# A hybrid decoder block on one core: the first layer norm's residuals, PSUM banks and POOL's row work rearranged

## The chip, the cores and the metric

The kernel runs on one core of a Trainium2 chip. Its engines are TensorE (PE in the profile: matrix products, with its weight loads on a row PEld), VectorE (DVE), ScalarE (ACT), GpSimd (POOL) and SyncE (SP, which here only issues DMAs). The metric is the device time of one execution in microseconds; the figure of a kernel is the median of its runs.

## The reference

One decoder layer for 256 tokens of 1024 features, float32. The change touches the end of the mixing part and the start of the feed-forward part (FFN):

```python
x = layer_norm(ALPHA * x + y @ w_out, ln1_g, ln1_b)       # mean and variance over 1024 features
u = causal_dwconv(x @ ffn_w_up, ffn_conv_w) + ffn_conv_b   # 3 taps along the tokens, 2 * 2816 columns
u_gate, u_val = split(u, 2)
f = (silu(u_gate) * u_val) @ ffn_w_down
x = layer_norm(ALPHA * x + f, ln2_g, ln2_b)
```

Ahead of that, `y` is the gated sum of a gated delta rule and a sparse attention over the same tokens.

## The kernel before

**Products.** Each float32 operand is split into a high part (`hi`, rounded to the type fp32r) and a low part (`lo`, what is left), and a product is done as three: hi by hi, hi by lo, lo by hi. Weights come from memory in chunks of 128x1024 (512 KB) in the order of a list, `PLAN`, through six buffers `raw`. `split_chunk` makes the parts: ACT casts `raw` to `hi` (L187) and DVE subtracts (L192); for some chunks POOL does a share of the subtraction (L194). `ahead()` splits the chunks that come next, as long as no more than three pairs (`hi`, `lo`) are in use; its argument `most` limits how many. Two sorts of chunks don't count: those with a place of their own (`alt`), and the first FFN pair `ug` 0 and `uv` 0 (`plain`), which is multiplied unsplit.

**Order.** Everything is unrolled, and each engine runs its own instructions in the order of the program. An instruction waits only for the data or the buffer that it needs from another engine. A DMA is issued by its engine's queue in the same way.

**Out projection (L1115 to L1141).** The result is two row tiles (`t`, 128 tokens each) by two halves of 512 features (`hf`), four PSUM tiles `pwo` from a pool `s` of four buffers. Eight chunks `wo` follow each other: four for half 0 with both row tiles, then four for half 1 with row tile 0 (L1141), and the same four with row tile 1 (three at L1187, the last at L1192). `resid` (L1130, L1131) adds ALPHA times the input row to the product, into `res` (tile NQ), and takes its statistics. It is called for (0, half 0) and (1, half 0) at L1139, and for half 1 inside `norm1`.

**First norm (L1172 to L1206).** `norm1(t)` finishes row tile t's statistics and normalizes half of it on DVE (L1174) and half on ACT. `trans1` transposes the row tile on TensorE into two PSUM tiles `pxt` of the pool `s` (L1154). `evac1` scales and shifts them into `x1T` (tile AT; DVE at L1162, ACT at L143), and `hilo1` makes the parts for the FFN (cast on ACT L1169, difference L1170 on POOL, for one piece on DVE). `first_up` (L1183) is the product of the unsplit pair with one row tile; its two results `pg0` lie in the two buffers of the PSUM pool `g`. At the end POOL scales and shifts the normalized rows for the second residual, `x1` (L1205, L1206): four operations of 128x1024. They read `res` and the tile KD; `x1` is read first after the FFN. SP's load of the second norm's constants (L1209) stands behind them in the program.

**FFN (L1244 to L1272).** 22 rounds j. A round multiplies two chunks, `ug` and `uv`, with all tokens (24 products each, L316 to L318, result in the pool `g`), convolves each (ACT takes the first tap at L143, DVE the two others at L349, reading PSUM and SBUF), and splits further chunks. ACT applies SiLU, DVE multiplies the two (L1263), ACT casts the result (L1267), DVE makes its low part (L1268). Then `down(j - 1)` (L1227 to L1229) multiplies the result of the round before with chunk `dn`, 15 products into five PSUM tiles, four from the pool `s` and one from the pool `o` of one buffer. The pool `c` has one buffer too; the attention was the last to use it.

Of the kernel before, what the change touches and what calls it, by code (L numbers as in the profile page):

```python
# [6 lines left out]
F32 = mybir.dt.float32  # L7
# [3 lines left out]
OP = mybir.AluOpType  # L11
# [85 lines left out]
class Body:  # L97
# [894 lines left out]
    def run(self):  # L992
        nc, A = self.nc, self.A
# [80 lines left out]
        xk = V.rearrange("p h t -> p (h t)").rearrange("p (t d) -> p t d", t=2)  # L1074
# [9 lines left out]
        lnp = self.KD.rearrange("p u j -> p (u j)")[:, :2048].rearrange("p (n d) -> p n d", n=2)  # L1084
# [23 lines left out]
        res = self.NQ.rearrange("p h t -> p (h t)").rearrange("p (t d) -> p t d", t=2)  # L1108
        x1 = self.LT[:, :2048].rearrange("p (t d) -> p t d", t=2)
        x1T = self.AT[:, 0:2048].rearrange("p (k t) -> p k t", k=8)  # L1110
        pw = {}
# [3 lines left out]
        def wo_mm(hf, i, ts):  # L1115
            if (hf, i) not in ch:
                ch[hf, i] = [c.rearrange("p (k n) -> p k n", k=2) for c in self.next_chunk("wo", 4 * hf + i)]
            hi, lo = ch[hf, i]
            for t in ts:
                self.mm_tok([pw[t, hf]], hi, lo, Y, 2 * i, i == 0, i == 3, t)  # L1120
            if ts[-1] == 1:
                self.done_chunk("wo", 4 * hf + i)
                if hf == 0:
                    self.ahead()

        def resid(t, hf, x, p):
            sl = slice(512 * hf, 512 * hf + 512)
            if hf == 0:
                bn[t] = self.work.tile([128, 2, 6], F32, name="bn", bufs=2)
            nc.vector.scalar_tensor_tensor(res[:, t, sl], x[:, t, sl], ALPHA, p[t, hf], op0=OP.mult, op1=OP.add)  # L1130
            nc.vector.bn_stats(bn[t][:, hf], res[:, t, sl])  # L1131

        for hf in range(2):
            for t in range(2):
                pw[t, hf] = self.ps("pwo")
        for i in range(4):
            wo_mm(0, i, (0, 1))
        for t in range(2):
            resid(t, 0, xk, pw)  # L1139
        for i in range(4):  # L1140
            wo_mm(1, i, (0,))  # L1141
        g1, b1 = self.pp("g1"), self.pp("b1")

        def stats1(t):
            resid(t, 1, xk, pw)
            return self.ln_stats(bn[t])
# [20 lines left out]
        def hilo1(t, k0, n, eng):  # L1167
            ts, ks = slice(128 * t, 128 * t + 128), slice(k0, k0 + n)
            nc.scalar.copy(X[:, 0, ks, ts], x1T[:, ks, ts])  # L1169
            eng.tensor_tensor(X[:, 1, ks, ts], x1T[:, ks, ts], X[:, 0, ks, ts].bitcast(F32), op=OP.subtract)  # L1170

        def norm1(t):  # L1172
            rs, nm = stats1(t)
            nc.vector.tensor_scalar(res[:, t, :512], res[:, t, :512], rs, nm, op0=OP.mult, op1=OP.add)  # L1174
            self.act(res[:, t, 512:], res[:, t, 512:], AF.Identity, scale=rs, bias=nm)

        pg0 = [self.ps_g() for _ in range(2)]

        def first_up(w, t):
            wt = up0[w].rearrange("p (k m) -> p k m", k=8)  # L1180
            ts = slice(128 * t, 128 * t + 128)
            for k in range(8):
                nc.tensor.matmul(pg0[w][:, ts], wt[:, k], x1T[:, k, ts], start=(k == 0), stop=(k == 7))  # L1183

        norm1(0)
        for i in range(WO_T):
            wo_mm(1, i, (1,))  # L1187
        p0 = trans1(0, (0, 1))
# [12 lines left out]
        evac1(1, 1, p1[1], nc.vector)  # L1201
        for q in range(2):
            hilo1(1, 4 * q, 4, (nc.gpsimd, nc.vector)[q])
        for t in range(2):
            nc.gpsimd.tensor_tensor(x1[:, t], res[:, t], lnp[:, 0], op=OP.mult)  # L1205
            nc.gpsimd.tensor_tensor(x1[:, t], x1[:, t], lnp[:, 1], op=OP.add)  # L1206

        ln2 = self.AT[:, 2048:4096].rearrange("p (n d) -> p n d", n=2)
        nc.sync.dma_start(ln2.rearrange("p n d -> p (n d)"),  # L1209
# [13 lines left out]
        def down_mm(j, n):  # L1223
            (hi, lo), (fh, fl), (t, o, w) = dch[j], fs[j], parts[n]
            ts, sl = slice(128 * t, 128 * t + 128), slice(o, o + w)
            p = pd[n][:, :w]
            nc.tensor.matmul(p, fh[:, ts], hi[:, sl], start=(j == 0), stop=False)  # L1227
            nc.tensor.matmul(p, fh[:, ts], lo[:, sl], start=False, stop=False)  # L1228
            nc.tensor.matmul(p, fl[:, ts], hi[:, sl], start=False, stop=(j == NFF - 1))  # L1229

        def down(j, ns=range(5)):
            if j == 0:
                for n in range(4):
                    pd[n] = self.ps("pdn")
                pd[4] = self.psum.tile([128, 512], F32, name="pdn", tag="o", bufs=1)
            if j not in dch:
                dch[j] = self.next_chunk("dn", j)
            for n in ns:
                down_mm(j, n)
            if ns[-1] == 4:  # L1240
                self.done_chunk("dn", j)
                self.ahead(most=1 if j > NFF - 4 else 3)

        for j in range(NFF):  # L1244
            uu = []
            for w, n in enumerate(("ug", "uv")):
                if j:
                    hi, lo = self.next_chunk(n, j)
                    pg = self.mm_feat(hi, lo, X)
                    self.done_chunk(n, j)  # L1250
                else:
                    first_up(w, 1)
                    self.done_chunk(n, 0)
                    pg = pg0[w]
                c = w * NFF + j
                u = self.scr(n)[:, :256]
                self.conv(pg, u, fcw[:, c], fcb[:, c:c + 1])
                uu.append(u)
                if j + w < NFF:
                    self.ahead(most=1 if j > NFF - 4 else 3)  # L1260
            self.act(uu[0], uu[0], AF.Silu)
            f = uu[0]
            nc.vector.tensor_tensor(f, uu[0], uu[1], op=OP.mult)  # L1263
            if j == NFF - 1:
                self.ahead(most=1)
            fh, fl = Y[:, 0, j % 5], Y[:, 1, j % 5]
            nc.scalar.copy(fh, f)  # L1267
            nc.vector.tensor_tensor(fl, f, fh.bitcast(F32), op=OP.subtract)  # L1268
            fs[j] = (fh, fl)
            self.ahead(most=1 if NFF - 1 > j > NFF - 4 else 3)  # L1270
            if 0 < j < NFF - 4:
                down(j - 1)  # L1272
        self.tab(AF.Exp)
        N = NFF
        last = range(N - 5, N)
# [188 lines left out]
```

## Time and profile before

| | |
|---|---|
| median of 3 runs | 586.69 us (585.82 to 587.82) |
| profiled execution: its span, the only time given of it | 585.1 us |
| TensorE busy | 565.1 us (97%) |
| VectorE busy | 395.9 us (68%) |
| ScalarE busy | 301.8 us (52%) |
| GpSimd busy | 110.7 us (19%) |

The span runs from the first to the last instruction; the time of a run includes what lies around it. Busy time of TensorE is modelled, and its products overlap: one starts before the one ahead of it has ended. In a line of a view, `out<-in` names the tiles, `xN` is the number of instructions merged into it, and the square bracket holds the idle time of that engine just before and what ended it. Times in the timelines are from the span's start.

### The profile page before, as it was taken

To read this page: it belongs to the slowest core of one execution; us is meant where nothing else is said; L and a number is where in the kernel's file an instruction comes from. 1 tells how busy PE (TensorE), PEld (TensorE's weight loads), DVE (VectorE), ACT (ScalarE), POOL (GpSimd) and SP (SyncE) were. 2 spreads that over 40 slices of the span, in tenths; PEclk is the share of its full clock that TensorE was granted. 3 is DMA by queue.
4 is the path that set the end of the run, shared out by engine and by line. 5 is a ranking of instruction groups with operands and counts; after the bars stand their busy time and mean duration, and the time that the engine had idled before them with its cause. 6 is when DMAs were issued, how large, how long until landed. Compare 5 with 4: busy or idle time off the path is not lost.

```text
span 585.1 us, 11569 instructions
## 1 busy us (share of the span) xinstructions
PE 565.1 (97%) x4588; PEld 510.4 (87%) x4588; DVE 395.9 (68%) x674; ACT 301.8 (52%) x550; POOL 110.7 (19%) x127
## 2 busy tenths in 40 slices
PE   8999999999989999999999999969999999999993
PEld 6999988878989998878979898769999999999983
DVE  1888743684986643576666486787777677777886
ACT  3655643424464475555685344355555555555651
POOL 1466611406310120020000000171000000000053
PEclk9999999999999999999999999998999999999998
DMA  8975578874953242323445455544555555555501
GB/s 267 408 253 173 171 233 263 298 231 148 273 168 103 85 134 79 102 73 109 146 146 169 162 183 194 190 135 130 190 188 187 180 184 190 192 189 183 181 2 72
DMA packets 29798, 101.87 MB, mean 174 GB/s; under 512 B 3536, under 2 KB 5360, under 8 KB 29360
## 3 DMA queue, kind: packets, MB, share of 16 engines
q1 hardware_dynamic: 28704, 96.85, 49.3%
q0 software_dynamic: 896, 3.95, 2.5%
q8 instruction: 36, 0.59, 0.4%
q10 hardware_dynamic: 144, 0.33, 0.1%
q14 instruction: 18, 0.15, 0.1%
HBM read 98.87 MB, written 1.46 MB: 171 GB/s over the span
## 4 chain that ended last, share of the span: by engine, by line
PE 77%; DVE 11%; ACT 5%; DMA 4%; issue 1%; SPq 0%; DVEq 0%; ACTq 0%
PE pg L316 18%; PE pg L318 17%; PE pg L317 17%; DVE lo L192 4%; DMA raw<-in_w 4%; PE pdn L1228 3%; PE pdn L1227 3%; PE pdn L1229 3%; ACT hi L187 2%; PE poa L925 2%; PE ph L779 1%; PE psa L865 1%; ACT AT L143 1%; DMA misc<-in_xT 1%; PE pvt L966 1%
## 5 line engine op out<-in xcount | busy, mean ns | idle before, releaser
L192 DVE TENSOR_TENSOR lo<-raw,hi 128x1024 fp32r<-128x1024 f32 (+2 forms) x149 | 182.1, 1222 | 87.7 <-ACT hi L187 86.9
L187 ACT CAST hi<-raw 128x1024 fp32r<-128x1024 f32 (+1 forms) x153 | 156.9, 1029 | 43.3 <-PE pg L317 13.4
L316 PE MATMUL pg<-X,hi 128*128 128x256 f32 x496 | 144.1, 291 | 2.6 <-DVE Z L349 1.7
L318 PE MATMUL pg<-X,lo 128*128 128x256 f32 x496 | 139.8, 282 | 0.3 <-DVE lo L192 0.3
L317 PE MATMUL pg<-X,hi 128*128 128x256 f32 x496 | 139.6, 281 | 0.0
L316 PE MATMUL pg<-Y,hi 128*128 128x256 f32 x400 | 114.3, 286 | 3.9 <-DVE uv L349 3.5
L317 PE MATMUL pg<-Y,hi 128*128 128x256 f32 x400 | 113.7, 284 | 0.0
L318 PE MATMUL pg<-Y,lo 128*128 128x256 f32 x400 | 113.6, 284 | 0.0
L316 PEld LDWEIGHTS pg<-X,hi 128*128 128x128 f32 x496 | 93.4, 188 | 11.7 <-issue 7.3
L318 PEld LDWEIGHTS pg<-X,lo 128*128 128x128 f32 x496 | 93.4, 188 | 0.7 <-DVE lo L192 0.5
L317 PEld LDWEIGHTS pg<-X,hi 128*128 128x128 f32 x496 | 93.5, 188 | 0.2 <-issue 0.2
L316 PEld LDWEIGHTS pg<-Y,hi 128*128 128x128 f32 x400 | 76.4, 191 | 4.5 <-issue 4.0
L317 PEld LDWEIGHTS pg<-Y,hi 128*128 128x128 f32 x400 | 76.4, 191 | 0.3 <-issue 0.2
L318 PEld LDWEIGHTS pg<-Y,lo 128*128 128x128 f32 x400 | 76.4, 191 | 0.0
L194 POOL TENSOR_TENSOR lo<-raw,hi 128x256 fp32r<-128x256 f32 (+1 forms) x21 | 19.9, 947 | 180.3 <-ACT hi L187 180.3
L1228 PE MATMUL pdn<-lo,X 128*128 128x512 f32 (+1 forms) x100 | 35.0, 350 | 0.7 <-DVE lo L192 0.7
L1227 PE MATMUL pdn<-hi,X 128*128 128x512 f32 (+1 forms) x100 | 35.1, 351 | 0.0
L1229 PE MATMUL pdn<-hi,X 128*128 128x512 f32 (+1 forms) x100 | 34.9, 349 | 0.0
L349 DVE SCALAR_TENSOR_TENSOR uv<-pg,ppk,uv 128x255 f32<-128x255 f32 (+1 forms) x44 | 21.2, 482 | 14.7 <-ACT uv L143 13.7
L349 DVE SCALAR_TENSOR_TENSOR cv<-pg,ppk,cv 128x255 f32<-128x255 f32 (+2 forms) x48 | 23.1, 481 | 7.9 <-ACT cv L143 6.8
L886 POOL TENSOR_SCALAR AT<-AT,sums 128x128 f32<-128x128 f32 (+1 forms) x12 | 11.2, 952 | 87.5 <-DVE sums L878 51.0
L143 ACT ACTIVATE uv<-pg,ppk 128x256 f32<-128x256 f32 x22 | 12.4, 565 | 28.1 <-PE pg L318 28.1
(323 smaller groups left out, 904.2 us busy)
## 6 DMA issues: line engine op xcount, KB each, us to landing
raw<-in_w SPq DMA_DIRECT2D x156, 512.0 KB, 3.3
AT<-in_w SPq DMA_DIRECT2D x16, 512.0 KB, 6.7
misc<-in_xT SPq DMA_DIRECT2D x4, 256.0 KB, 4.5
raw<-in_w SPq DMA_DIRECT2D x8, 128.0 KB, 4.2
LT<-rscr POOLq DMA_DIRECT2D x2, 512.0 KB, 8.3
V<-in_xk POOLq DMA_DIRECT2D x1, 1024.0 KB, 5.5
KD<-in_lnp POOLq DMA_DIRECT2D x1, 1024.0 KB, 5.9
AT<-in_lnp SPq DMA_DIRECT2D x1, 1024.0 KB, 7.7
```

Of the source, the lines that this page charges most:

```text
L143: self.nc.scalar.activation(out, in_, func, **kw)
L187: nc.scalar.copy(hi[:, o:o + n], raw[:, o:o + n])
L192: nc.vector.tensor_tensor(lo[:, :n], raw[:, :n], hi[:, :n].bitcast(F32), op=OP.subtract)
L194: nc.gpsimd.tensor_tensor(lo[:, n:], raw[:, n:], hi[:, n:].bitcast(F32), op=OP.subtract)
L316: nc.tensor.matmul(pg, hi[:, k], src[:, 0, k], start=(k == 0), stop=False)
L317: nc.tensor.matmul(pg, hi[:, k], src[:, 1, k], start=False, stop=False)
L318: nc.tensor.matmul(pg, lo[:, k], src[:, 0, k], start=False, stop=(k == 7))
L349: nc.vector.scalar_tensor_tensor(dst[:, s:], pg[:, :S - s], cw[:, n - 1 - s:n - s], dst[:, s:], op0=OP.mult, op1=OP.add)
L925: nc.tensor.matmul(po, self.VT[:, b % 2, c0:c0 + 128], PT[:, b].rearrange("p i q -> p (i q)"), start=False, stop=(b == bs[-1]))
L1227: nc.tensor.matmul(p, fh[:, ts], hi[:, sl], start=(j == 0), stop=False)
L1228: nc.tensor.matmul(p, fh[:, ts], lo[:, sl], start=False, stop=False)
L1229: nc.tensor.matmul(p, fl[:, ts], hi[:, sl], start=False, stop=(j == NFF - 1))
```

## The change

The residual of row tile 0's first half comes ahead of the split of chunk `ug` 1, that of row tile 1's first half behind `norm1(0)`, and the four `pwo` tiles are taken in the order row tile by row tile. The two results of `first_up` are put into the pools `o` and `c` rather than `g`. POOL's scale and shift of the rows are cut into eight pieces of 256 features of a row tile, two instructions each (16 instructions of 128x256 rather than four of 128x1024), and a piece stands behind each of the FFN rounds 2 to 9 in the program.

```diff
@@ wo_mm
                 self.done_chunk("wo", 4 * hf + i)
-                if hf == 0:
+                if hf == 0 and i < 3:
                     self.ahead()
@@ out projection
-        for hf in range(2):
-            for t in range(2):
+        for t in range(2):
+            for hf in range(2):
                 pw[t, hf] = self.ps("pwo")
         for i in range(4):
             wo_mm(0, i, (0, 1))
-        for t in range(2):
-            resid(t, 0, xk, pw)
+        resid(0, 0, xk, pw)
+        self.ahead(most=1)
         for i in range(4):
             wo_mm(1, i, (0,))
@@ first norm
-        pg0 = [self.ps_g() for _ in range(2)]
+        pg0 = [self.psum.tile([128, 512], F32, name="pg", tag=t, bufs=1)[:, :256] for t in "oc"]
@@
         norm1(0)
+        resid(1, 0, xk, pw)
         for i in range(WO_T):
             wo_mm(1, i, (1,))
@@
-        for t in range(2):
-            nc.gpsimd.tensor_tensor(x1[:, t], res[:, t], lnp[:, 0], op=OP.mult)
-            nc.gpsimd.tensor_tensor(x1[:, t], x1[:, t], lnp[:, 1], op=OP.add)
+
+        def affine1(n):
+            t, sl = n // 4, slice(256 * (n % 4), 256 * (n % 4) + 256)
+            nc.gpsimd.tensor_tensor(x1[:, t, sl], res[:, t, sl], lnp[:, 0, sl], op=OP.mult)
+            nc.gpsimd.tensor_tensor(x1[:, t, sl], x1[:, t, sl], lnp[:, 1, sl], op=OP.add)
@@ FFN rounds
             if 0 < j < NFF - 4:
                 down(j - 1)
+            if 1 < j < 10:
+                affine1(j - 2)
```

## Rows read from the trace of the kernel before

**Rows 1.** Windows: stretch, length, busy us of PE, PEld, DVE, ACT, POOL, clock, DMA.

```profile
392.50:399.30 6.80, 5.71 (x26) 5.64 (x27) 6.15 (x8) 1.96 (x4) 4.70 (x2) 0.50 0.26 80
399.40:560.00 160.60, 160.60 (x1211) 154.00 (x1210) 119.23 (x175) 89.45 (x136) 3.59 (x2) 1.00 0.55 181
```

**Rows 2.** TensorE's longest wait from 352 to 560: total, times, longest.

```profile
PE pg L316 <- DVE uv L349: 3.5, 1, 3.5
```

**Rows 3.** Timeline of TensorE: start, duration, line, tiles, idle before.

```profile
373.18 0.39 PE L968 MATMUL pwo<-YD,X 128*128 128x512 f32 x1
374.63 1.09 PE L1154 MATMUL pxt<-cpk,NQ 128*128 128x128 f32 x8 [1.06 <-DVE NQ L1174]
...
386.96 0.36 PE L316 MATMUL pg<-Y,hi 128*128 128x256 f32 x1 [0.38 <-DVE ug L349]
...
389.77 0.28 PE L318 MATMUL pg<-Y,lo 128*128 128x256 f32 x1
393.59 0.55 PE L316 MATMUL pg<-Y,hi 128*128 128x256 f32 x1 [3.55 <-DVE uv L349]
...
398.85 0.61 PE L1227 MATMUL pdn<-hi,X 128*128 128x512 f32 x1
...
401.88 0.28 PE L316 MATMUL pg<-Y,hi 128*128 128x256 f32 x1
...
407.58 0.39 PE L1227 MATMUL pdn<-hi,X 128*128 128x512 f32 x1
...
410.38 0.28 PE L316 MATMUL pg<-Y,hi 128*128 128x256 f32 x1
```

**Rows 4.** Timeline of DVE in FFN rounds 0 and 1.

```profile
386.74 5.80 DVE L192 TENSOR_TENSOR lo<-raw,hi 128x1024 fp32r<-128x1024 f32 x2
392.46 0.99 DVE L349 SCALAR_TENSOR_TENSOR uv<-pg,ppk,uv 128x255 f32<-128x255 f32 x2
393.55 1.49 DVE L1263 TENSOR_TENSOR ug<-ug,uv 128x256 f32<-128x256 f32 x1
395.51 2.05 DVE L1268 TENSOR_TENSOR X<-ug,X 128x256 fp32r<-128x256 f32 x1 [0.47 <-ACT X L1267]
...
400.69 1.22 DVE L192 TENSOR_TENSOR lo<-raw,hi 128x1024 fp32r<-128x1024 f32 x1
...
402.72 0.43 DVE L1268 TENSOR_TENSOR X<-ug,X 128x256 fp32r<-128x256 f32 x1 [0.47 <-ACT X L1267]
```

**Rows 5.** Timeline of POOL from the last difference to its last row operation.

```profile
384.09 1.27 POOL L1170 TENSOR_TENSOR Y<-AT,Y 128x512 fp32r<-128x512 f32 x1 [3.97 <-ACT Y L1169]
385.32 2.83 POOL L1205 TENSOR_TENSOR LT<-NQ,KD 128x1024 f32<-128x1024 f32 x1
...
394.83 2.45 POOL L1206 TENSOR_TENSOR LT<-LT,KD 128x1024 f32<-128x1024 f32 x1
```

**Rows 6.** Timeline of DVE around the out projection's residuals.

```profile
367.33 1.23 DVE L192 TENSOR_TENSOR lo<-raw,hi 128x1024 fp32r<-128x1024 f32 x1 [1.65 <-ACT hi L187]
368.47 0.68 DVE L1130 SCALAR_TENSOR_TENSOR NQ<-V,pwo 128x512 f32<-128x512 f32 x1
...
371.11 0.67 DVE L1130 SCALAR_TENSOR_TENSOR NQ<-V,pwo 128x512 f32<-128x512 f32 x1
...
375.76 1.37 DVE L1162 TENSOR_SCALAR AT<-pxt,ppk 128x128 f32<-128x128 f32 x4 [1.19 <-PE pxt L1154]
```

**Rows 7.** Timeline of SP's queue: the load of the second norm's constants.

```profile
366.09 0.42 SPq L1209 DMA_DIRECT2D AT<-in_lnp  x1
```

**Rows 8.** Instructions of L194: least, median, longest ns, first and last start.

```profile
L194 POOL TENSOR_TENSOR lo<-raw,hi x21: 734/739/1796, 15.7 to 565.5; 128x256 fp32r<-128x256 f32 x17, 128x512 fp32r<-128x512 f32 x4
```

**Rows 9.** Timeline of ACT: cast of round 0's result, split of chunk dn 1.

```profile
395.07 0.41 ACT L1267 CAST X<-ug 128x256 fp32r<-128x256 f32 x1 [5.60 <-DVE ug L1263]
...
402.60 1.04 ACT L187 CAST hi<-raw 128x1024 fp32r<-128x1024 f32 x1
```

**Rows 10.** Windows, as rows 1: a stretch in the middle of the kernel.

```profile
160.00:164.00 4.00, 2.28 (x20) 2.10 (x19) 3.89 (x7) 1.25 (x3) 1.24 (x1) 1.00 0.68 171
```

## The prediction

> **What bounds the kernel now.** I read the page first (TensorE is busy for 97% of the span), then the windows after the out projection, then TensorE's waits, and last the timelines of TensorE, VectorE (DVE), POOL and ACT there. From 399.4 to 560 us TensorE is busy for all of 160.60 us while DVE has 41 us to spare [rows 1]: time won before 399.4 goes through to the end, and nothing is to be won behind it. What is lost lies between 373 and 402. The largest wait of TensorE there is the second matrix of FFN round 1, which waits 3.5 us for the convolution of "uv" on DVE [rows 2]. The timeline shows what is lost [rows 3]: 1.06 us idle ahead of the transposes at 374.63, 0.38 at 386.96, 3.55 at 393.59, and then a slow stretch: the granted clock is 0.50 (1.2 GHz) from 392.5 to 399.3 and 1.00 (2.4 GHz) afterwards [rows 1]. TensorE had stood idle since 390.05 (389.77 + 0.28). The 24 products from 393.59 to 398.85 take 5.26 us; the 48 from 401.88 to 407.58 take 5.70, so 24 at full clock take 2.85. The "down" group takes 3.03 (398.85 to 401.88), later 2.80 (407.58 to 410.38).
>
> **Why DVE is late.** Its two splits at 386.74 take 5.80 us, a clean one takes 1.22; the product at 393.55 takes 1.49 and the difference at 395.51 2.05, where one of that size takes 0.43 clean (402.72) [rows 4]. In the same time POOL runs the four 1024-column operations of L1205 and L1206, back to back from 385.32 to 394.83 + 2.45 [rows 5]. They alternate: POOL's first ends at 388.15 (385.32 + 2.83), and a split of 1.22, one POOL operation of 2.25 (the 2.45 at 394.83 less some 0.2 of waiting) and the other split lead to 392.84, where the pair ends at 392.54; there is no room for two POOL operations in a row. DVE's L349, which reads PSUM, is not lengthened (0.99 for two). So DVE loses (5.80 - 2.44) + 1.06 + 1.62 = 6.04 us here.
>
> **The reordered residuals.** Now DVE makes the low part of chunk ug1 (367.33, waiting for its cast) ahead of both residuals of the first half, so the residual of row tile 0's second half starts at 371.11 [rows 6]. Two residuals with their statistics take 371.11 - 368.47 = 2.64 us, so one 1.32. Afterwards the first residual stands ahead of that split (in the 1.65 us that DVE sat idle before 367.33), and the one of row tile 1 behind the norm. The split still ends at 368.56, and the residual starts when its product ends: the last of its 24 products stands 18 x 0.23 us before 373.18, at 369.0, and ends at 369.4 (a "down" group is nine products of 512 columns and six of 256 at 0.12: (2.80 - 0.72)/9 = 0.23). That is 1.67 us sooner; the transposes could start at 374.63 - 1.67 = 372.96. TensorE's queue reaches them at 373.41: the product at 373.18 lasts 0.39, and products follow each other 0.16 us before the end (one of 256 columns is 0.28 long, and one starts each 5.70/48 = 0.12). **Gain 1.06 + 0.16 = 1.22 us**, bounds 1.06 and 1.22. The moved residual falls into DVE's wait for these transposes: 372.95 to 374.3, while the first column block to be evicted is ready 375.76 - 374.63 = 1.13 us after the transposes' start [rows 3, 6], at 374.54. Without that cover the evictions would come up to 1.3 us later, and row tile 0's first FFN products behind them. PSUM order follows: the four tiles are reused in the order in which they become free. The rest up to 386.3, the second transposes' short wait too, moves 1.22 us forward unchanged.
>
> **The other PSUM banks.** The pair of round 0 leaves the two buffers that round 1 uses. So ug1 no longer waits for L349 of round 0: 0.38 + 0.16 = **0.54 us**. And uv1 no longer waits for "uv" of round 0: 3.55 + 0.16 = **3.71 us**, and with it goes the clock's fall: (5.26 - 2.85) + (3.03 - 2.80) = **2.64 us**. What is late next: uv1 needs its own split (first in DVE's queue), then down(0) needs round 0's product, cast and difference, which pass through all of DVE's delayed operations. The last "down" buffer shares a bank with ug of round 0, which DVE has read some 5 us before.
>
> **POOL's 16 instructions.** They stand in the program behind eight rounds, but nothing they read comes from a round: rows, scale and shift are there before round 0. A queue here does not wait for its place in the program: SP issued L1209, which stands behind all the first norm's work, at 366.09 [rows 7]. So I expect them to run one after the other from about 384.1, when POOL's last split ends (384.09 + 1.27 - 1.22), as the four do now. What changes is the length of one hold of POOL. Bounds: a quarter of those 2.25 us is 0.56; the same shape and kind in L194 takes 0.734 at least [rows 8]. I take 0.65, between the two. An operation of DVE with both inputs in SBUF then waits for one piece at most.
>
> DVE after the change: free at 386.74 - 1.22 = 385.52. Split of uv1 385.95 to 387.15, of dn0 387.8 to 389.0, L349 to 390.0, product 390.3 to 390.7, ACT's cast 0.41 [rows 9] to 391.2, difference 391.35 to 391.8. TensorE: ug1 from 385.2 (386.96 - 0.54 - 1.22), uv1 from 388.05 to 390.9 with its split in time. Down(0) then waits 0.3 for the cast and 0.15 to 0.2 for the difference: **0.5 us lost**. ug2 starts at 394.2, uv2 ends at 399.85, both splits ready. In round 1 DVE does L349 twice (1.0 each), splits of ug2 and uv2, product and difference, each of the four SBUF operations with up to 0.65 us of waiting, to 398.9; the cast of dn1 comes after ACT's cast of the product (1.04, [rows 9]) and the split of dn1 ends at 400.75, where down(1)'s second product wants it at 400.1: **0.67 us lost**. Then POOL is done (16 pieces, about 404) and DVE's 2 us of slack in a round of 8.5 take over.
>
> Bounds of these two losses: none, if the pieces fall between DVE's operations; and 2.3 + 2.1 = 4.4 if each operation waits a full 0.74: round 0's chain is then 4 x 0.74 + 2.44 + 0.99 + 0.43 + 0.41 + 0.43 = 7.66 from 385.52, so 393.2 against 390.9; round 1's, with a third split, 5 x 0.74 + 3.66 + 1.98 + 0.86 + 0.41 = 10.6 from there, so 403.8 against the need, then at 401.7.
>
> The Trainium skill (SBUF — State Buffer, Who interferes with whom) states that of a VectorE instruction with two SBUF inputs and a GpSimd instruction that reads SBUF the later one is blocked until the earlier has finished. The trace agrees with the block (5.80 for the two splits against 2.44), and the rule speaks against the cut: POOL's total hold stays, and if DVE stood at all 16 pieces it would lose 16 x 0.65 = 10.4 us rather than 6.04, over two rounds; that would put the time near the upper end of the range, 583. It says nothing of who is next when both wait.
>
> **Sum.** 1.22 + 0.54 + 3.71 + 2.64 - 0.5 - 0.67 = 6.94, say 7.0 us. The span of 585.1 becomes 578.1. The page gives no other time for the profiled execution; the median of the runs (586.69) is 1.6 us above the span, and that stays: 586.69 - 7.0 = **579.7 us**.
>
> **Rivals.**
> (A) The pieces really are spread over eight rounds, by a wait I don't see. Then round 0 on DVE is clean, f is ready by 390.4, before 390.9, and both losses vanish: gain 8.11, 578.6 us. For it: a wait for a buffer or a counter would not show in a trace without those instructions. Against: SP's early issue, and POOL's operations today follow each other with no wait but DVE's.
> (B) The stop moves to down(0) and the clock falls again. A stop of some 3 us there and 2.64 lost to the clock leave 8.11 - 5.64 = 2.5 us gain: 584.2 us. For it: DVE's chain ends within 1 us of the need and each piece may cost more than 0.74. Against: TensorE stood idle for 1.72 of the 4 us from 160 on (4.00 - 2.28), and the granted clock was 1.00 there [rows 10].
> (C) Slower: POOL keeps DVE's two-input operations out from piece to piece, and they get in only after the last, at 384.7 + 16 x 0.65 = 395.1. uv1's split ends at 396.3 where TensorE wants it at 388.3; it stops for 8 us and runs uv1 at half clock to about 401.6, where down(0) started at 398.85 before: 2.7 us slower, 589.4. It decides from about eleven pieces in a row on. Against: each of DVE's four delayed operations today came in after one POOL operation.
> (D) No change: the time is lost again on some later wait. Against: 160.60 us without one.
>
> **Chances.** My forecast 0.63, A 0.13, B 0.14, C 0.06, D 0.04. About 0.3% (1.8 us) is what a measurement of this kernel can tell from no change. Faster: 0.63 + 0.13 + 0.14 = 0.90, within 0.04, slower 0.06. Range: 578.2 (8.11 and a little that products overlap) to 583.0 (8.11 - 4.4 = 3.7 gained); it leaves out B's far half, C and D.
>
> **What will show it.** Right: transposes follow the out projection with no idle; round 1's two matrices without a stop between them; clock 1.00 throughout; idle of 0.3 to 1 us ahead of the "down" groups of rounds 0 and 1; POOL's 16 operations of 0.6 to 1.9 us back to back from 384 to about 404; DVE's splits there at most 0.74 us over 1.22. Wrong: POOL's pieces 8.5 us apart (A), a clock of 0.5 after 390 (B), a split of many pieces' length (C), or the first transposes still waiting for L1174.

## The result, and the profile after

The changed kernel takes 580.19 us (median of 4 runs, 578.40 to 581.23), the kernel before, measured with it, 586.83. The ratio is 0.9876 with an interval of 0.9848 to 0.9903: 7.3 us by the ratio (5.7 to 8.9), where 7.0 were forecast. The profiled execution is the quickest of the four (578.40, span 576.6).

The span is 8.5 us shorter, but not all of it is the change's. The first product of the out projection starts 0.65 us sooner, in a part of the program that is the same in both. So I use the *stretch* from there to the first product of the last "down" group, which also leaves out the end. The timelines of TensorE give it; first before, then after:

```profile
352.54 0.39 PE L966 MATMUL pwo<-hi,X 128*128 128x512 f32 x1
...
560.57 0.40 PE L1227 MATMUL pdn<-YD,X 128*128 128x512 f32 x1
```

```profile
351.88 0.39 PE L966 MATMUL pwo<-hi,X 128*128 128x512 f32 x1
...
552.08 0.40 PE L1230 MATMUL pdn<-YD,X 128*128 128x512 f32 x1
```

208.03 us became 200.20: **7.83 us**, where the sum of my steps was 6.94. The windows of the changed kernel (columns as in rows 1) answer to [rows 1]:

```profile
384.00:400.00 16.00, 16.00 (x121) 15.03 (x121) 14.21 (x20) 10.52 (x17) 15.45 (x15) 1.00 0.59 195
391.00:560.00 169.00, 168.31 (x1244) 159.85 (x1243) 129.23 (x187) 95.82 (x145) 20.66 (x16) 1.00 0.53 173
```

From 384 to 400 TensorE is busy throughout, at a granted clock of 1.00, beside a POOL that is busy for 15.45 of the 16 us. The clock stays at 1.00 up to 560 us, behind the last "down" group's start. The timeline of TensorE there answers to [rows 3]:

```profile
372.52 0.40 PE L968 MATMUL pwo<-YD,X 128*128 128x512 f32 x1
372.76 1.04 PE L1154 MATMUL pxt<-cpk,NQ 128*128 128x128 f32 x8
...
390.07 0.28 PE L318 MATMUL pg<-Y,lo 128*128 128x256 f32 x1
390.22 0.50 PE L1230 MATMUL pdn<-hi,X 128*128 128x512 f32 x1
...
393.14 0.28 PE L316 MATMUL pg<-Y,hi 128*128 128x256 f32 x1
...
398.83 0.39 PE L1230 MATMUL pdn<-hi,X 128*128 128x512 f32 x1
399.21 0.50 PE L1231 MATMUL pdn<-lo,X 128*128 128x512 f32 x1
...
401.88 0.28 PE L316 MATMUL pg<-Y,hi 128*128 128x256 f32 x1
```

The transposes follow 0.24 us after the start of the product ahead of them, without idle time. The two matrices of round 1 run into each other. Down(0) takes 2.92 us (393.14 - 390.22) and down(1) 3.05, against 2.80 in [rows 3]: 0.12 and 0.25 us more, where I had 0.5 and 0.67.

DVE in rounds 0 and 1 answers to [rows 4]:

```profile
384.81 3.35 DVE L192 TENSOR_TENSOR lo<-raw,hi 128x1024 fp32r<-128x1024 f32 x2
388.08 0.99 DVE L349 SCALAR_TENSOR_TENSOR uv<-pg,ppk,uv 128x255 f32<-128x255 f32 x2
389.17 0.56 DVE L1266 TENSOR_TENSOR ug<-ug,uv 128x256 f32<-128x256 f32 x1
390.20 0.43 DVE L1271 TENSOR_TENSOR X<-ug,X 128x256 fp32r<-128x256 f32 x1 [0.47 <-ACT X L1270]
...
391.61 1.52 DVE L192 TENSOR_TENSOR lo<-raw,hi 128x1024 fp32r<-128x1024 f32 x1
...
393.95 1.67 DVE L192 TENSOR_TENSOR lo<-raw,hi 128x1024 fp32r<-128x1024 f32 x1
395.55 0.96 DVE L1266 TENSOR_TENSOR ug<-ug,uv 128x256 f32<-128x256 f32 x1
...
397.93 1.23 DVE L192 TENSOR_TENSOR lo<-raw,hi 128x1024 fp32r<-128x1024 f32 x1 [0.53 <-ACT hi L187]
```

The two splits take 3.35 us rather than 5.80, the product 0.56 rather than 1.49, the difference 0.43 rather than 2.05. And POOL, of which these are five of its 16 instructions (rows 5 has those before):

```profile
383.39 1.18 POOL L1208 TENSOR_TENSOR LT<-NQ,KD 128x256 f32<-128x256 f32 x1
384.65 0.74 POOL L1209 TENSOR_TENSOR LT<-LT,KD 128x256 f32<-128x256 f32 x1
385.36 1.72 POOL L1208 TENSOR_TENSOR LT<-NQ,KD 128x256 f32<-128x256 f32 x1
387.15 1.59 POOL L1209 TENSOR_TENSOR LT<-LT,KD 128x256 f32<-128x256 f32 x1
...
400.54 1.60 POOL L1209 TENSOR_TENSOR LT<-LT,KD 128x256 f32<-128x256 f32 x1
```

They run back to back from 383.39 to 402.14, while DVE works on rounds 0 to 2, and not over eight rounds: each starts within 0.1 us of the end of the one ahead of it, and none waits for anything that a round makes. What does keep them a round apart is shown by e6.

### The profile page after: what moved, and what is told of

It is laid out like the page before. It is cut to its first block, busy times and chain, and to the rows that moved or that the text cites. A ratio compares the mean times of both kernels' runs of the same rounds, so it can differ in the third digit from the quotient of the medians.

```text
span 576.6 us, 11581 instructions
## 1 busy us (share of the span) xinstructions
PE 561.4 (97%) x4588; PEld 507.2 (88%) x4588; DVE 391.8 (68%) x674; ACT 301.6 (52%) x550; POOL 115.4 (20%) x139
## 4 chain that ended last, share of the span: by engine, by line
PE 79%; DVE 10%; ACT 6%; DMA 3%; issue 1%; SPq 0%; DVEq 0%; ACTq 0%
PE pg L316 18%; PE pg L318 17%; PE pg L317 17%; PE pdn L1231 3%; PE pdn L1230 3%; PE pdn L1232 3%; DVE lo L192 3%; PE ph L779 2%; DMA raw<-in_w 2%; PE poa L925 2%; ACT hi L187 2%; DMA VN<-tscr 1%; PE pwo L967 1%; PE pwo L968 1%; PE pwo L966 1%
## 5 line engine op out<-in xcount | busy, mean ns | idle before, releaser
L316 PE MATMUL pg<-Y,hi 128*128 128x256 f32 x400 | 113.0, 283 | 0.0
L317 PE MATMUL pg<-Y,hi 128*128 128x256 f32 x400 | 112.7, 282 | 0.0
L317 PEld LDWEIGHTS pg<-Y,hi 128*128 128x128 f32 x400 | 75.3, 188 | 0.3 <-issue 0.2
L316 PEld LDWEIGHTS pg<-Y,hi 128*128 128x128 f32 x400 | 75.3, 188 | 0.2 <-issue 0.2
L194 POOL TENSOR_TENSOR lo<-raw,hi 128x256 fp32r<-128x256 f32 (+1 forms) x21 | 19.8, 946 | 167.6 <-ACT hi L187 167.6
L1270 ACT CAST X<-ug 128x256 fp32r<-128x256 f32 x22 | 8.9, 407 | 33.5 <-DVE ug L1266 33.5
```

Of the source, the lines that this page charges most:

```text
L194: nc.gpsimd.tensor_tensor(lo[:, n:], raw[:, n:], hi[:, n:].bitcast(F32), op=OP.subtract)
L316: nc.tensor.matmul(pg, hi[:, k], src[:, 0, k], start=(k == 0), stop=False)
L317: nc.tensor.matmul(pg, hi[:, k], src[:, 1, k], start=False, stop=False)
```

## The experiments

Theory H: TensorE was stopped by DVE, which POOL's long operations kept out, and the shared banks only set where TensorE met it. The rivals stand with each run. Each ratio is to the kernel before, measured beside the run; each stretch is that of the one profiled execution. The times of a kernel's runs spread over 1.5 to 6.5 us, while the stretches of e6 and e7, where POOL is out of the way in two different manners, agree to 0.01 us, and what follows the stretch takes 24.5 to 24.6 us in all eleven profiles; so I read small effects from the stretch. But where the clock falls, or TensorE waits for work that hangs on a DMA, the stretch itself differs between executions, by up to 1.3 us (e1 and e3). That touches every difference from the kernel before, and not those among the changed kernel and e5 to e9.

| run | ratio to before, interval | stretch, us | against before |
|---|---|---|---|
| before | 1 | 208.03 | |
| after | 0.9876, 0.9848 to 0.9903 | 200.20 | -7.83 |
| e1 banks alone | 0.9999, 0.9974 to 1.0023 | 206.93 | -1.10 |
| e2 pieces alone | 0.9928, 0.9899 to 0.9956 | 203.03 | -5.00 |
| e3 residuals alone | 0.9974, 0.9952 to 0.9996 | 205.46 | -2.57 |
| e4 all but the pieces | 1.0005, 0.9985 to 1.0026 | 206.27 | -1.76 |
| e5 pieces of 512 | 0.9909, 0.9874 to 0.9943 | 200.88 | -7.15 |
| e6 pieces a round apart | 0.9889, 0.9858 to 0.9920 | 199.79 | -8.24 |
| e7 no pieces | 0.9870, 0.9842 to 0.9898 | 199.79 | -8.24 |
| e8 a difference on DVE | 0.9867, 0.9835 to 0.9898 | 199.71 | -8.32 |
| e9 e6 and e8 | 0.9879, 0.9849 to 0.9908 | 199.31 | -8.72 |

**e1, the banks alone.**

```diff
-        pg0 = [self.ps_g() for _ in range(2)]
+        pg0 = [self.psum.tile([128, 512], F32, name="pg", tag=t, bufs=1)[:, :256] for t in "oc"]
```

> The kernel before with the two results of first_up in the pools o and c, nothing else; POOL keeps its four operations of 128x1024. Theory H (what stops TensorE is DVE, kept out by POOL's long holds; the banks only set where TensorE meets it): uv of round 1 no longer waits for L349 and runs from 389.3 to 392.1, but the difference of round 0's result still ends near 397.5, so TensorE stops for some 4 to 5 us ahead of down(0) instead, the clock falls to 0.50 there, and the time is that of before: 586.8, between 585.5 and 588. Theory B (the shared banks are the cause, POOL's operations a bystander): most of the gain is there, about 6.3 us: 580.5, and no stop longer than 1 us.

587.36 us: no difference. The timeline of TensorE in this kernel shows where the stop went:

```profile
399.07 0.79 PE L1227 MATMUL pdn<-hi,X 128*128 128x512 f32 x1 [3.29 <-ACT X L1267]
401.14 0.79 PE L1229 MATMUL pdn<-hi,X 128*128 128x512 f32 x1 [0.85 <-DVE X L1268]
```

A window of it shows the clock:

```profile
398.10:404.80 6.70, 4.88 (x12) 3.49 (x13) 6.16 (x8) 3.62 (x6) 2.62 (x2) 0.50 0.19 64
```

The wait for the bank is gone and the wait for round 0's result has taken its place: 3.29 us for the cast, 0.85 for the difference, and the products behind them run at half clock. Theory B is out.

Of the 1.10 us by which the stretch is shorter, 0.99 lie ahead of the first transposes, in a part that this edit does not touch: they start 21.10 us after the out projection's first product (378.13 - 357.03) rather than 22.09. The cast of chunk `ug` 1, which waits for its DMA, started 12.72 us after that product (369.75 - 357.03) and in the kernel before 13.70 (366.24 - 352.54). The lines of e1's TensorE and ACT, then of ACT before:

```profile
378.13 1.09 PE L1154 MATMUL pxt<-cpk,NQ 128*128 128x128 f32 x8
369.75 1.05 ACT L187 CAST hi<-raw 128x1024 fp32r<-128x1024 f32 x1 [1.21 <-DMA raw<-in_w]
```

```profile
366.24 1.05 ACT L187 CAST hi<-raw 128x1024 fp32r<-128x1024 f32 x1 [2.19 <-DMA raw<-in_w]
```

So the idle time of 1.06 us that the reordered residuals remove is there in some executions of the old order and gone in others, with the time at which that chunk is cast.

**e2, the pieces alone.** The kernel before with `affine1` and its calls as in the change's diff; banks and residuals as before.

> The kernel before with POOL's scale and shift in 16 instructions of 128x256, nothing else; banks and residuals as before. Theory H: DVE's two splits take about 3.4 us rather than 5.8, L349 of uv ends near 391, TensorE waits about 1.1 us rather than 3.55 and the clock stays at 1.00: gain 2.45 + 2.6 = 5.0 us, 581.8 (580.8 to 583). Theory B: uv of round 1 still shares its bank with round 0, so the stop stays and the time is that of before, 586 to 587.5.

583.06 us, just above the range, and the stretch is 5.00 us shorter, as worked out. TensorE's waits from 345 to 420 in this kernel:

```profile
PE pxt L1154 <- DVE NQ L1174: 1.6, 2, 1.1
PE pg L316 <- DVE uv L349: 1.1, 1, 1.1
PE pg L316 <- DVE ug L349: 0.4, 1, 0.4
```

The 3.55 us have become 1.1 with the banks still shared, and the clock stays at 1.00 there. The shared banks still cost these 1.1 and 0.4 us; that they "only set where TensorE met" the late DVE is too strong.

**e3, the residuals alone.** The kernel before with `i < 3`, the order of `pwo`, `ahead(most=1)` and the two moved calls of `resid`.

> The kernel before with the residuals reordered (and the order of the four pwo tiles), nothing else. Both theories: the idle of 1.06 us ahead of the first transposes goes, all behind it is as before but 1.2 us earlier, the stop of 3.5 us and the half clock too: 585.6 (584.8 to 586.4). If the reordering were worth more (the rest of the stretch hangs on it), under 584.

585.76 us, as expected. The idle time ahead of the first transposes is gone, the 3.55 us wait and the half clock remain. The stretch shortens by 2.57 us rather than 1.2. The rest is in the clock, which came back sooner in this execution: round 1's second matrix took 4.19 us rather than 5.26 and down(0) 2.80 rather than 3.03. From TensorE's timeline:

```profile
395.20 0.55 PE L316 MATMUL pg<-Y,hi 128*128 128x256 f32 x1 [3.55 <-DVE uv L349]
...
399.39 0.39 PE L1228 MATMUL pdn<-hi,X 128*128 128x512 f32 x1
...
402.19 0.28 PE L316 MATMUL pg<-Y,hi 128*128 128x256 f32 x1
```

The same stop of 3.55 us thus cost 1.34 us of clock here (4.19 - 2.85) and 2.64 in the profile of the kernel before. That 1.3 us is no gain of the edit.

**e4, all but the pieces.**

```diff
-        def affine1(n):
...
+        for t in range(2):
+            nc.gpsimd.tensor_tensor(x1[:, t], res[:, t], lnp[:, 0], op=OP.mult)
+            nc.gpsimd.tensor_tensor(x1[:, t], x1[:, t], lnp[:, 1], op=OP.add)
```

> The changed kernel with POOL's four operations of 128x1024 put back. Theory H: as e1 and 1.2 us sooner: a stop of 4 to 5 us ahead of down(0) and the clock at 0.50 there: 585.6 (584.3 to 587). Theory B: within 0.5 us of the changed kernel, 580.2.

587.11 us, just above the upper end of what H gave, and no gain that the times show. TensorE's waits, as in e1:

```profile
PE pdn L1228 <- ACT X L1268: 3.2, 1, 3.2
PE pdn L1230 <- DVE X L1269: 1.3, 1, 1.3
```

Together these two parts are worth nothing in the time without the third (1.0005, 0.9985 to 1.0026), though the residuals alone were worth 0.2 to 2.8 us in e3. The stretch is 1.76 us shorter, as far as one execution tells.

**e5, pieces of 512.**

```diff
-            t, sl = n // 4, slice(256 * (n % 4), 256 * (n % 4) + 256)
+            t, sl = n // 2, slice(512 * (n % 2), 512 * (n % 2) + 512)
...
-            if 1 < j < 10:
+            if 1 < j < 6:
```

> The changed kernel with POOL's scale and shift in 8 instructions of 128x512 rather than 16 of 128x256. Theory H (what a DVE operation with two SBUF inputs loses is the length of the one POOL piece it meets, 1.2 us here against 0.74): DVE's two splits of round 0 take 4.2 to 4.6 us, round 0's difference ends 2 to 2.7 us later than in the changed kernel, and TensorE stops for 1.5 to 2.5 us ahead of down(0); without the clock's fall 1.8 to 2.8 us slower than the changed kernel (582 to 583), with it up to 5. Theory S (POOL's total hold counts, however it is cut): within 1 us of e4, 586 to 587. Theory N (any cut is enough): within 0.5 us of the changed kernel.

581.73 us; the stretch is 0.68 us longer than the changed kernel's. That is a miss: less than H gave, far from S, and in the stretch 0.18 us more than N allows; the times (0.9909 and 0.9876, with intervals that overlap) can't tell it from N. TensorE's one wait there is 0.3 us, for round 0's difference. The reason stands in the timelines of DVE and POOL of this run:

```profile
386.17 3.63 DVE L192 TENSOR_TENSOR lo<-raw,hi 128x1024 fp32r<-128x1024 f32 x2
...
390.82 0.42 DVE L1266 TENSOR_TENSOR ug<-ug,uv 128x256 f32<-128x256 f32 x1
391.71 0.95 DVE L1271 TENSOR_TENSOR X<-ug,X 128x256 fp32r<-128x256 f32 x1 [0.47 <-ACT X L1270]
```

```profile
384.75 1.74 POOL L1208 TENSOR_TENSOR LT<-NQ,KD 128x512 f32<-128x512 f32 x1
386.57 2.15 POOL L1209 TENSOR_TENSOR LT<-LT,KD 128x512 f32<-128x512 f32 x1
388.68 2.27 POOL L1208 TENSOR_TENSOR LT<-NQ,KD 128x512 f32<-128x512 f32 x1
```

An operation of DVE waited for what was left of the piece that ran, not always for a whole one. The first split starts at 386.17, shortly before POOL's piece ends (384.75 + 1.74 = 386.49), and loses 0.2 us; the second meets nearly a whole piece and loses 1.1; the product meets none, since POOL got through its third piece while DVE read PSUM. Round 0 loses (3.63 - 2.44) + 0 + 0.52 = 1.7 us, where I had put 1.8 to 2.2 on the splits alone.

**e6, pieces really a round apart.**

```diff
+        tick = self.small(1, "tick")
-        def affine1(n):
+        def affine1(n, gate):
             t, sl = n // 4, slice(256 * (n % 4), 256 * (n % 4) + 256)
+            nc.gpsimd.tensor_copy(tick, gate)
...
-                affine1(j - 2)
+                affine1(j - 2, f[:, :1])
```

> The changed kernel with a POOL copy of one column ahead of each piece's two instructions, which reads that round's product: so POOL's pieces really run one round apart. Theory H: rounds 0 and 1 are free of POOL, both remaining losses ahead of the down groups (0.1 and 0.25 us in the changed kernel) vanish, each later round loses less than its 2 us of slack: 0.3 to 0.4 us faster than the changed kernel, which the times can't tell apart; the stretch from the out projection to the last down group shortens by 0.3 to 0.4 us. Rival: the pieces in rounds 2 to 9 each delay a split that TensorE wants, and the time grows by up to 8 x 0.5 us.

The stretch is 0.41 us shorter than the changed kernel's; the times (580.94 us) can't tell. One piece (two instructions) follows round 2's product, with 6.74 us of idle time ahead of the next:

```profile
407.10 0.19 POOL L1209 COPY tick<-ug 128x1 f32<-128x1 f32 x1 [18.67 <-DVE ug L1268]
407.24 0.74 POOL L1210 TENSOR_TENSOR LT<-NQ,KD 128x256 f32<-128x256 f32 x1
408.06 0.80 POOL L1211 TENSOR_TENSOR LT<-LT,KD 128x256 f32<-128x256 f32 x1
415.59 0.18 POOL L1209 COPY tick<-ug 128x1 f32<-128x1 f32 x1 [6.74 <-DVE ug L1268]
```

**e7, no pieces.** The calls and the function are left out.

> The changed kernel without POOL's scale and shift: leaves out the computation of x1, so the second residual reads what lies in its place. Theory H: what POOL still costs is the 0.35 us ahead of the down groups of rounds 0 and 1; DVE's splits take 1.22 each; 0.3 to 0.5 us faster than the changed kernel. Rival: DVE's delays by POOL still cost TensorE 1 us or more (my forecast said 1.17).

This kernel leaves out `x1` and only times what is left. The stretch is 199.79 us, the same as e6 to 0.01: all that the pieces still cost in the changed kernel is 0.41 us, and spread over eight rounds they cost nothing.

**e8, the second difference of row tile 0 on DVE.** `hilo1`'s subtraction becomes a function `low1` of its own, and the second one moves:

```diff
         for q in range(2):
-            hilo1(0, 4 * q, 4, nc.gpsimd)
+            hilo1(0, 4 * q, 4, (nc.gpsimd, None)[q])
         up0 = [self.next_chunk(n, 0) for n in ("ug", "uv")]
         norm1(1)
+        low1(0, 4, 4, nc.vector)
```

> The changed kernel with the second of POOL's two differences for row tile 0 put on DVE, behind the normalization of row tile 1 (the cast stays where it is). Theory H: DVE's L980 no longer meets that POOL operation (0.70 us becomes 0.22), and the idle of 0.48 us ahead of the second transposes goes; the difference of 0.69 us lies in DVE's wait for these transposes (1.19 us): 0.4 to 0.5 us faster than the changed kernel in the stretch, hardly to be told in the times. Rival: the idle stays, because the transposes wait for ACT's half or for something else than L980; no change.

L980, a step of the statistics on 128x1, took 0.71 us in the changed kernel, because it met POOL's operation. The lines, first of DVE and POOL in the changed kernel, where L980 ends with POOL's two differences (377.51 + 0.71 and 375.69 + 2.51), then of DVE in e8:

```profile
375.69 2.51 POOL L1170 TENSOR_TENSOR Y<-AT,Y 128x512 fp32r<-128x512 f32 x2 [53.42 <-ACT Y L1169]
377.51 0.71 DVE L980 SCALAR_TENSOR_TENSOR mv<-mv 128x1 f32<-128x1 f32 x1
```

```profile
378.46 0.22 DVE L980 SCALAR_TENSOR_TENSOR mv<-mv 128x1 f32<-128x1 f32 x1
```

The idle time ahead of the second transposes is gone, and the stretch is 0.49 us shorter: as H had it.

**e9, e6 and e8 together.**

> The changed kernel with e6 and e8 together: POOL's pieces really one round apart, and the second difference of row tile 0 on DVE. Theory H: the two are independent, so the stretch from the out projection to the last down group shortens by 0.41 + 0.49 = 0.9 us, to 199.3 us; no idle ahead of the second transposes, none ahead of the down groups of rounds 0 and 1. In the times 0.9 us (0.15%) is under what can be told: median 578.5 to 581, about 1.3% under the kernel before. Rival: the two gains are one (both from less meeting of DVE and POOL) and the stretch stays at 199.7.

The stretch is 199.31 us, 0.89 less than the changed kernel's: the two add up. The median of 579.77 us is clearly under the kernel before, but not to be told from the changed kernel's 580.19.

## Why the prediction was right

- **The reordered residuals.** 1.22 us forecast. From the first product of the out projection the transposes started 22.09 us on (374.63 - 352.54) and now 20.88 on (372.76 - 351.88): 1.21 us. e3 shows it alone (376.30 - 355.41 = 20.89). The size hangs on the execution of the old order, though: e1's, with that order, needed 21.10, so against it the edit would have been worth 0.2.
- **The other banks and the clock.** 0.54 + 3.71 + 2.64 us forecast. Both waits and the half clock are gone. But the step gives the banks what belongs to two edits: e1 and e4 show that the banks without the pieces move the stop to down(0), and e2 that the pieces without the banks take away 5.00 of the 6.89 us. The two go together; my sum was that of both, and the text named the banks for all of it. For the banks 7.83 - 5.00 - 1.21 leaves some 1.6 us once the pieces are short, by subtraction and not by a run. And that 2.64 for the clock fits is partly luck: it is what one execution paid, and e3's paid 1.34 for the same stop.
- **POOL back to back.** Right: 383.39 to 402.14. A piece that met no DVE operation took 0.73 to 0.80 us, more than the 0.65 that I took and near the end of 0.734 that [rows 8] gave.
- **The new losses.** 0.5 + 0.67 = 1.17 us forecast, 0.12 + 0.25 = 0.37 measured, 0.41 by e6 and e7. This is the term that was mis-sized; the places were right, down(0) behind the cast and down(1)'s second product behind the split of dn1. In round 0 I had let DVE's four operations wait for POOL for 1.5 us together (0.43 and 0.65 the splits, 0.3 the product, 0.15 the difference). The splits lost 3.35 - 2.44 = 0.91 us and the product 0.14, the difference nothing. In round 1 the two splits lost 0.30 and 0.45 and the product 0.54, 1.3 us and about what my times hold; there the chain only started earlier. My chain of times also left out that an operation of DVE starts some 0.1 us before the one ahead of it ends (388.08 against 384.81 + 3.35 = 388.16). e5 fits this: what counted was the rest of the piece that ran at that moment, and while DVE read PSUM POOL got on. The pieces themselves were longer than I had taken, which worked the other way.
- **The sum.** 8.11 - 0.37 = 7.74 us; the stretch gives 7.83. The time shows less (586.83 - 580.19 = 6.64 by the medians, 7.3 by the ratio), and by the ratio it does so in all ten runs, by 0.5 to 2.1 us. Executions differ by a few us before the out projection: its first product starts between 351.88 and 357.03 us in the eleven profiles, and nothing of the change lies ahead of it. And the stretch of the kernel before, 208.03 us, may be one of the longer ones, by its clock and its idle time ahead of the transposes; the record has no second profile of that kernel. So 7.83 is what two executions differ by, and 7.3 (5.7 to 8.9) is the figure for the change.
- **The rivals.** A, really spread pieces, did not come about; made to come about (e6), it is worth 0.41 us where I had given it 1.1 more than my forecast. B, the stop at down(0) with the clock's fall, is what e1 and e4 do; the short pieces kept the change from it. C would need POOL to go first twice; in the timelines shown no waiting operation of DVE let a second one past. The rule from the Trainium skill (SBUF — State Buffer, Who interferes with whom), that the later of the two is blocked until the earlier ends, held: in the changed kernel L980, begun at 377.51, ended at 378.22, with POOL's difference at 378.20. What I had drawn from it, that the cut alone might not help, did not: POOL's total became longer (16 x 0.74 = 11.8 us against four of 2.25), and DVE's loss in round 0 fell from 6.04 to 1.05.

## What to carry to other kernels

When an engine stops behind a queue of short operations, find out which operation there has grown, and beside what: here DVE's 1.22 us splits had become 2.9 next to POOL's operations of 128x1024. Cutting the off-path operation into pieces costs its own engine time and limits what any one operation beside it can lose. Lifting a buffer wait alone may only move the stop to the next consumer of the same late result; try each part of a change alone and all but each, since two of these three together were worth nothing that the times show until the third was there. And a gain read off one profile can hold the luck of that execution: read the same stop in a second one.

## What the runs showed of the hardware that I had not expected

The length of an idle stretch alone did not tell whether the clock falls. I had argued from 1.72 us of idle time without a fall [rows 10]. In e2 TensorE waited 1.40 us ahead of L796, in a part that no edit touches, and the clock was 0.50 from 118.0 to 121.3; in e3 it waited 2.90 us at the same place, and the clock stayed. TensorE's timeline and windows of e2:

```profile
116.73 0.63 PE L796 MATMUL phs<-cpk,hp 128*128 128x30 f32 x4 [1.40 <-DVE LT L531]
```

```profile
112.00:117.90 5.90, 4.50 (x48) 3.54 (x46) 3.79 (x5) 3.95 (x6) 2.74 (x2) 1.00 0.65 258
118.00:121.30 3.30, 3.30 (x16) 3.30 (x17) 3.27 (x6) 0.51 (x2) 0.00 (x0) 0.50 0.47 163
```

The same of e3:

```profile
119.28 0.63 PE L796 MATMUL phs<-cpk,hp 128*128 128x30 f32 x4 [2.90 <-DVE LT L531]
```

```profile
119.30:126.00 6.70, 6.70 (x72) 5.74 (x72) 6.00 (x9) 3.07 (x6) 0.00 (x0) 1.00 0.54 171
```

This wait runs from none in the changed kernel's profile to 2.90 us in e3's. The two profiles whose out projection starts latest, e1 (357.03) and e6 (356.88), waited 1.77 and 1.96 us there, and the clock fell in both. It is likely one source of the spread between executions; what makes it long in one and short in another was not tried.
